# Splitting and re-assigning the first steps of a two-layer transformer kernel's opening

## The chip, the cores and the metric

The kernel runs on one core of a Trainium2 chip. A core has a matrix engine (PE, with its weight loads shown apart as PEld), a vector engine (DVE), a scalar engine (ACT), a general engine (POOL) and a sync engine (SP) that issues most DMA transfers. Each engine executes its own instructions in the order in which they stand in the program, and waits on semaphores for the others. The metric is the device time of one execution in microseconds (us). Before the change it is 1490.43 us, the median of three runs (1489.74 to 1490.46).

## The reference, cut to what matters

The reference runs two layers over 1024 latent and 256 context tokens of width 1024, in fp32: a windowed grouped-query attention, then a latent attention. Only the very beginning of the first layer matters here: each token row is normalised by its root mean square, scaled and shifted channel by channel, and multiplied with the input weights.

```
shift_x, scale_x, gate_x = adaln(c, ada_w[i], ada_b[i])
hx = rms_norm(x, norm_g[i]) * (1.0 + scale_x[:, None]) + shift_x[:, None]
hc = rms_norm(ctx, norm_g[i]) * (1.0 + scale_c) + shift_c
...
q, k, v, g = jnp.split(h @ w_in, [A_WIDTH, A_WIDTH + A_KV_WIDTH, A_WIDTH + 2 * A_KV_WIDTH], axis=-1)
```

`silu(c) @ w` inside `adaln` gives the per-channel scale and shift, so that no row can be finished before part of `ada_w` has been loaded and multiplied.

## The kernel before, in words

Every fp32 operand of a large product is kept as two parts in a format that PE multiplies in one pass: a **high part** (the value cast) and a **low part** (the value less its high part). A product is then three matmuls: high by high, low by high, high by low.

Tokens are handled in five pairs of 128-token tiles: pair 0 is the context, pairs 1 to 4 the latent tokens. A pair and a group of two 128-channel blocks make one group of the opening; there are 20 of them, and for each the opening does the same things:

- `square(p)` (ACT, L863): the sum of squares of each of the two tiles, 128x1024 each, into an accumulator. `norm(p)`: a small DVE operation (L867) and a small power on POOL (L868) make the reciprocal root from both sums at once. `scale(p, j, eng)`: tile j is multiplied by it on DVE (L875) or on ACT (L873).
- `turn(p, b, bank)` (PE, L882): four transposes bring two channel blocks of the pair into one PSUM bank.
- `h_part(p, b, hi)`: DVE applies scale and shift from the bank into SBUF, one channel block of 256 columns at a time (L890, two per group); then `hi`, a cast by ACT or POOL, writes the high part of both blocks (L892, 128x512).
- `h_low(p, b, eng)` (L897): DVE or POOL subtracts to get the low part.
- `v_part(p, b)`: eight matmuls with the high part (L906), then four with the low part (L911), into the bank of the pair.

Between them stand pieces of the scale and shift computation: `ada_mm` (PE, L839), `ada_copy` (ACT, L844), `ada_cols` (PE, L849, and three small DVE operations on L328 and L331), and the cutting of the first weight block (`w0_cut`, L929 and L930). SP loads in a fixed order: context, `ada_w`, the first piece of weights, the four tiles of pairs 1 and 2, the second piece of weights, more of `ada_w`, then pair 3 and the rest.

The opening is written out by hand in program order and is issued exactly so; no planner reorders it. One further rule sets waits: instructions of two different engines that touch the same PSUM bank, even if both only read it, and even if they read different columns, are put in program order by a semaphore.

Of the kernel before, what the change touches and what calls it, by code (L numbers as in the profile page):

```python
# [14 lines left out]
AF = mybir.ActivationFunctionType  # L15
ALU = mybir.AluOpType
# [4 lines left out]
D = 1024  # L21
# [5 lines left out]
EPS = 1e-6  # L27
# [190 lines left out]
def kernel(ctx: ExitStack, tc: tile.TileContext, t, out, dbg=None):  # L218
    plan = Plan()
    nc = Recorder(tc.nc, plan)  # L220
# [75 lines left out]
    mhalf = sm(1)  # L296
# [563 lines left out]
    def square(p):  # L860
        junk = V[:, 8:10].rearrange("p a b c -> p (a b c)") if p > 2 else PB[:, 3:5, :].rearrange("p a b -> p (a b)")
        for j in range(2):
            nc.scalar.activation(junk, xn[p][0][:, j], AF.Square, accum_out=xn[p][1][:, j : j + 1])  # L863

    def norm(p):
        _, sq, st = xn[p]
        nc.vector.tensor_scalar(st[:, 0:2], sq[:, 0:2], 1.0 / D, EPS, ALU.mult, ALU.add)  # L867
        nc.gpsimd.tensor_tensor(st[:, 2:4], st[:, 0:2], mhalf.to_broadcast([128, 2]), ALU.pow)  # L868
# [8 lines left out]
    def turn(p, b, bank):  # L877
        tbank[p, b] = ps = shp(PB[:, bank, :], 2, 256)
        for kk in range(2):
            for j in range(2):  # L880
                c0 = (2 * b + kk) * 128
                nc.tensor.transpose(ps[:, kk, j * 128 : j * 128 + 128], xn[p][0][:, j, c0 : c0 + 128], ident)  # L882

    def h_part(p, b, hi=nc.scalar.copy):
        w = 1 if p == 0 else 0
        ps, h = tbank[p, b], shp(hr.next(), 2, 256)
        for kk in range(2):
            k = 2 * b + kk
            sa, sb = ada0.A[:, k, w : w + 1], ada0.B[:, k, w : w + 1]
            nc.vector.tensor_scalar(h[:, kk], ps[:, kk], sa, sb, ALU.mult, ALU.add)  # L890
        ks = slice(2 * b, 2 * b + 2)
        hi(hT[p][:, 0, ks, :], h)  # L892
        hs[p, b] = h
# [5 lines left out]
    def v_part(p, b):  # L899
        h, W = hT[p], wt[0]  # L900
        for j in range(2):
            js = slice(j * 128, j * 128 + 128)
            o = PB[:, p, j * 256 : j * 256 + 256]
            for k in (2 * b, 2 * b + 1):
# [70 lines left out]
    h_part(0, 0, nc.gpsimd.tensor_copy)  # L975
    square(1)
    norm(1)
    h_low(0, 0, nc.vector)
    for j in range(2):
        scale(1, j, nc.vector)  # L980
    v_part(0, 0)
    turn(1, 0, 7)
    square(2)
    norm(2)
    h_part(1, 0)
    scale(2, 0, nc.vector)
    scale(2, 1, nc.scalar)
# [7 lines left out]
    h_part(2, 0)  # L995
# [10 lines left out]
    h_part(0, 1, nc.gpsimd.tensor_copy)  # L1006
# [3 lines left out]
    h_part(1, 1)  # L1010
# [1100 lines left out]
```

## Time and profile before

| what | value |
|---|---|
| time, median of three runs | 1490.43 us |
| the profiled execution's own time | 1488.73 us |
| its span, first to last instruction | 1486.9 us |
| mean granted clock of PE | 0.997 |
| PE busy | 1462.6 us, 98% of the span |
| DVE, ACT, POOL busy | 1064.1, 733.5, 810.4 us |
| stretch 14 to 24 us: PE busy, granted clock | 7.05 of 10 us, 0.66 |
| stretch 28 to 36 us: PE busy | 6.99 of 8 us |
| stretch 48 to 60 us: PE busy | 12.00 of 12 us |

A row of the timeline gives start, duration, engine, line, operation, what it writes and reads, shape and count (consecutive instructions of one kind are merged); in brackets stands the idle time of that engine before it and what ended it. A row of groups gives the count, the busy time in us, the mean of one in ns, and the idle time before it. A row of the stretches gives the length, each engine's busy time, PE's granted clock and the DMA engines' share. A row of the waits reads: who waited, for whom, us in total, how often, the longest.

### The profile page before, as it was taken

What the parts mean: (1) busy time and instruction counts of PE and PEld (TensorE: products, weight loads), DVE (VectorE), ACT (ScalarE), POOL (GpSimd) and SP (SyncE); (2) the same over time, 40 slices, a digit from 0 to 9 for tenths busy, and PEclk for the clock granted to TensorE, in tenths of its full rate; (3) what the DMA queues carried; (4) which work ended last, traced back from release to release, by engine and by line L of the source; (5) the groups of instructions that cost most, each with busy time, mean ns of one, the idle gap of its engine ahead of it and who ended that gap; (6) DMA issues with size and microseconds to landing.
All of it is one profiled execution on the core that took longest, in us unless ns stands there. A gap on an engine that the chain in (4) does not pass through costs nothing.

```text
span 1486.9 us, 25072 instructions
## 1 busy us (share of the span) xinstructions
PE 1462.6 (98%) x9036; PEld 1188.3 (80%) x9036; DVE 1064.1 (72%) x2029; ACT 733.5 (49%) x1397; POOL 810.4 (55%) x735
## 2 busy tenths in 40 slices
PE   6999999999999999999999999999999999999998
PEld 4888888888888888888888888766777767876687
DVE  3787789738778888878988777666576466566764
ACT  4421222359888878876554432443454344444321
POOL 2563366346454444456300240798788788789371
PEclk9999999999999999999999999999999999999999
DMA  9545644673343333336444566011122212120442
GB/s 336 170 171 170 212 150 169 208 223 114 121 144 119 98 101 98 100 100 229 119 120 119 169 234 207 21 41 53 47 63 70 62 47 61 54 68 28 151 152 86
DMA packets 146964, 186.01 MB, mean 125 GB/s; under 512 B 12812, under 2 KB 100492, under 8 KB 146840
## 3 DMA queue, kind: packets, MB, share of 16 engines
q1 hardware_dynamic: 141864, 177.75, 37.7%
q10 hardware_dynamic: 4976, 6.66, 1.3%
q8 instruction: 71, 1.16, 0.3%
q14 instruction: 53, 0.43, 0.1%
HBM read 134.02 MB, written 46.15 MB: 121 GB/s over the span
## 4 chain that ended last, share of the span: by engine, by line
PE 49%; DVE 2%; issue 1%; DMA 0%; POOL 0%; ACT 0%; POOLq 0%; DVEq 0%; ACTq 0%
PE PB L1788 13%; PE PB L1811 9%; PE PB L285 7%; PE PB L287 7%; PE PB L286 7%; PE PB L1754 5%; PE PB L1822 1%; DVE arena_r L281 1%; DMA arena_r<-arena_f 0%; PE PB L1768 0%; DVE arena_f L1327 0%; DVE krF L1760 0%; DVE arena_f L1236 0%; DVE arena_f L1329 0%; DVE arena_f L1328 0%
## 5 line engine op out<-in xcount | busy, mean ns | idle before, releaser
L285 PE MATMUL PB<-arena_r 128*128 128x512 f32 (+2 forms) x1200 | 439.4, 366 | 1.3 <-DVE arena_f L1236 1.3
L286 PE MATMUL PB<-arena_r 128*128 128x512 f32 (+2 forms) x1200 | 433.7, 361 | 0.1
L287 PE MATMUL PB<-arena_r 128*128 128x512 f32 (+2 forms) x1200 | 433.3, 361 | 0.0
L1804 POOL TENSOR_TENSOR arena_f<-arena_f 128x1024 f32<-128x1024 f32 x120 | 285.9, 2382 | 8.2
L285 PEld LDWEIGHTS PB<-arena_r 128*128 128x128 f32 x1200 | 226.3, 189 | 45.7 <-issue 9.0
L287 PEld LDWEIGHTS PB<-arena_r 128*128 128x128 f32 x1200 | 226.3, 189 | 33.7
L286 PEld LDWEIGHTS PB<-arena_r 128*128 128x128 f32 x1200 | 226.5, 189 | 32.2 <-POOL arena_r L281 0.8
L1788 PE MATMUL PB<-arena_r 64*128 64x512 f32 (+1 forms) x1600 | 229.6, 395 | 0.0
L1798 ACT ACTIVATE arena_f<-PB 128x1024 f32<-128x1024 f32 x160 | 164.5, 1028 | 112.0 <-PE PB L1788 84.0
L1760 DVE TENSOR_REDUCE krF<-PB 128x1 f32<-128x512 f32 (+1 forms) x264 | 167.0, 678 | 65.7 <-PE PB L1754 65.6
L1788 PEld LDWEIGHTS PB<-arena_r 64*128 64x128 f32 (+1 forms) x1600 | 179.4, 185 | 14.7 <-issue 5.2
L704 DVE CUSTOM_DVE_ANT_0 arena_f<-PB,arena_f,small 128x256 f32<-128x256 f32 (+1 forms) x288 | 148.1, 525 | 51.9 <-PE PB L698 33.3
L280 ACT CAST arena_r<-PB 128x512 fp32r<-128x512 f32 (+2 forms) x207 | 115.3, 564 | 113.2 <-PE PB L287 73.3
L281 DVE TENSOR_TENSOR arena_r<-PB,arena_r 128x512 fp32r<-128x512 f32 (+2 forms) x207 | 134.3, 661 | 34.7 <-ACT arena_r L280 34.1
L1811 PE MATMUL PB<-arena_f 128*64 128x512 f32 x640 | 145.9, 595 | 0.0
L281 POOL TENSOR_TENSOR arena_r<-arena_f,arena_r 128x512 fp32r<-128x512 f32 (+1 forms) x64 | 87.9, 1388 | 102.9 <-ACT arena_r L280 89.4
L710 ACT ACTIVATE arena_f<-arena_f,small 128x640 f32<-128x640 f32 (+2 forms) x160 | 119.1, 745 | 15.8 <-DVE small L704 13.6
L280 ACT CAST arena_r<-arena_f 128x512 fp32r<-128x512 f32 (+1 forms) x142 | 82.2, 611 | 87.3 <-PE PB L287 28.3
L507 DVE SCALAR_TENSOR_TENSOR arena_f<-arena_f,small 128x512 f32<-128x512 f32 x98 | 114.0, 1208 | 10.9 <-DMA arena_f<-ada_w 10.6
L737 PE MATMUL PB<-arena_r 128*128 128x512 f32 x336 | 118.6, 429 | 0.0
L1754 PE MATMUL PB<-arena_r 64*128 64x512 f32 (+1 forms) x768 | 114.2, 355 | 0.1
L727 PE MATMUL PB<-ident,arena_f 128*128 128x128 f32 x672 | 108.6, 272 | 0.1
(215 smaller groups left out, 2087.2 us busy)
## 6 DMA issues: line engine op xcount, KB each, us to landing
arena_f<-ada_w SPq DMA_DIRECT2D x96, 256.0 KB, 4.1
arena_r<-q_d SPq DMA_DIRECT2D x160, 128.0 KB, 2.8
arena_f<-a_w_in SPq DMA_DIRECT2D x40, 256.0 KB, 3.9
arena_f<-b_w_in SPq DMA_DIRECT2D x36, 256.0 KB, 2.9
arena_f<-x SPq DMA_DIRECT2D x16, 512.0 KB, 5.8
q_d<-arena_f SPq DMA_DIRECT2D x16, 512.0 KB, 3.0
arena_r<-qn_d SPq DMA_DIRECT2D x16, 512.0 KB, 5.0
g_d<-arena_f ACTq DMA_DIRECT2D x20, 256.0 KB, 3.7
```

The costliest lines, as they stand in the source:

```text
L280: nc.scalar.copy(hi, src)
L281: (lo_eng or nc.vector).tensor_sub(lo, src, hi.bitcast(F32))
L285: nc.tensor.matmul(o, ah, bh, start=first, stop=False)
L286: nc.tensor.matmul(o, al, bh, start=False, stop=False)
L287: nc.tensor.matmul(o, ah, bl, start=False, stop=last)
L704: nc.vector.tensor_tensor_reduce(o, S, mk, -A_SCALE, prev, ALU.add, ALU.min, mx)
L1754: nc.tensor.matmul(bank[:, o : o + n], self.q[r, s, bs], k[r, 0, n0 : n0 + n], start=s == 0, stop=s == 2)
L1760: nc.vector.reduce_max(self.mxp[:, e, b : b + 1, i], bank[:, 0:n], AX.X)
L1788: nc.tensor.matmul(PB[:, b + e, :], k[r, s, cs], q[r, sq], start=i == 0, stop=i == 4)
L1798: nc.scalar.activation(E, PB[:, b : b + 2, :], AF.Exp)
L1804: eng.tensor_add(acc, acc, E)
L1811: nc.tensor.matmul(PB[r, 7, :], Vq[:, c, h, :], E[:, e], start=c == 0, stop=c == NT - 1)
```

## The change

Five edits, all in the opening:

1. `square` and `norm` can be called for one tile. For pairs 1 and 2 the power is now taken tile by tile, each tile is scaled as soon as its own power is there, and both tiles of pair 2 are scaled on DVE (the second was on ACT).
2. `turn` issues the two transposes of the first tile before those of the second; `v_part` issues the high matmuls channel block by channel block.
3. The high part of group (0, 0) is cast on POOL in two halves, one channel block each.
4. Four high parts no longer go through SBUF: ACT computes scale and shift itself, with the scale and shift columns as its operands, from the PSUM bank into the high part (`hi is None`), one channel block at a time, for (1, 0), (0, 1) and (1, 1) with two instructions each. DVE still computes the same from the same bank into SBUF, for the low part. Before, (1, 0) and (1, 1) were cast by ACT and (0, 1) by POOL.
5. The high part of (2, 0) is cast by POOL instead of ACT.

Three calls of `h_part` pass `None`, which makes six ACT instructions.

```diff
-    def norm(p):
+    def norm(p, j=0, n=2):
         _, sq, st = xn[p]
-        nc.vector.tensor_scalar(st[:, 0:2], sq[:, 0:2], 1.0 / D, EPS, ALU.mult, ALU.add)
-        nc.gpsimd.tensor_tensor(st[:, 2:4], st[:, 0:2], mhalf.to_broadcast([128, 2]), ALU.pow)
+        nc.vector.tensor_scalar(st[:, j : j + n], sq[:, j : j + n], 1.0 / D, EPS, ALU.mult, ALU.add)
+        nc.gpsimd.tensor_tensor(st[:, 2 + j : 2 + j + n], st[:, j : j + n], mhalf.to_broadcast([128, n]), ALU.pow)
...
-        for kk in range(2):
-            for j in range(2):
+        for j in range(2):
+            for kk in range(2):
                 c0 = (2 * b + kk) * 128
                 nc.tensor.transpose(ps[:, kk, j * 128 : j * 128 + 128], xn[p][0][:, j, c0 : c0 + 128], ident)
 
-    def h_part(p, b, hi=nc.scalar.copy):
+    def h_part(p, b, hi=nc.scalar.copy, parts=1):
...
             nc.vector.tensor_scalar(h[:, kk], ps[:, kk], sa, sb, ALU.mult, ALU.add)
+            if hi is None:
+                nc.scalar.activation(hT[p][:, 0, k], ps[:, kk], AF.Identity, bias=sb, scale=sa)
+            elif parts == 2:
+                hi(hT[p][:, 0, k], h[:, kk])
         ks = slice(2 * b, 2 * b + 2)
-        hi(hT[p][:, 0, ks, :], h)
+        if hi and parts == 1:
+            hi(hT[p][:, 0, ks, :], h)
...
-    h_part(0, 0, nc.gpsimd.tensor_copy)
-    square(1)
-    norm(1)
-    h_low(0, 0, nc.vector)
+    h_part(0, 0, nc.gpsimd.tensor_copy, 2)
     for j in range(2):
+        square(1, [j])
+        norm(1, j, 1)
+        if j == 0:
+            h_low(0, 0, nc.vector)
         scale(1, j, nc.vector)
     v_part(0, 0)
     turn(1, 0, 7)
-    square(2)
-    norm(2)
-    h_part(1, 0)
+    square(2, [0])
+    norm(2, 0, 1)
+    square(2, [1])
+    h_part(1, 0, None)
     scale(2, 0, nc.vector)
-    scale(2, 1, nc.scalar)
+    norm(2, 1, 1)
+    scale(2, 1, nc.vector)
     w0_cut(1)
...
     h_low(1, 0, nc.vector)
     v_part(1, 0)
...
-    h_part(2, 0)
+    h_part(2, 0, nc.gpsimd.tensor_copy)
...
-    h_part(0, 1, nc.gpsimd.tensor_copy)
+    h_part(0, 1, None)
     square(3)
     h_low(0, 1, nc.vector)
     norm(3)
-    h_part(1, 1)
+    h_part(1, 1, None)
     h_low(1, 1)
```

Where instructions now stand is seen at three places. In these rows stand the line, the operation, what is written and read (`PB` is PSUM, `arena_f` and `arena_r` are SBUF, `small` holds the columns), the shape and the semaphores waited for. Up to L890 the line numbers are the same in both kernels; further down they are five higher in the changed one: L892 there is the new ACT instruction, L897 the 512-column cast and L902 the low part.

The first place is DVE from the scaling of pair 1 to the low part of group (1, 0). Before:

```order
L875 TENSOR_SCALAR arena_f<-arena_f,small 128x1024 [waits DMAHW0_49,Pool_49]
L875 TENSOR_SCALAR arena_f<-arena_f,small 128x1024 [waits DMAHW1_49]
L867 TENSOR_SCALAR small<-small 128x2 [waits Activation_49]
L890 TENSOR_SCALAR arena_f<-PB,small 128x256 [waits PE_49]
L890 TENSOR_SCALAR arena_f<-PB,small 128x256
L875 TENSOR_SCALAR arena_f<-arena_f,small 128x1024 [waits DMAHW2_49,Pool_49]
L897 TENSOR_TENSOR arena_r<-arena_f,arena_r 128x512 [waits Activation_49]
```

The same place now:

```order
L875 TENSOR_SCALAR arena_f<-arena_f,small 128x1024 [waits DMAHW0_49,Pool_49]
L867 TENSOR_SCALAR small<-small 128x1 [waits Activation_49]
L875 TENSOR_SCALAR arena_f<-arena_f,small 128x1024 [waits DMAHW1_49,Pool_49]
L867 TENSOR_SCALAR small<-small 128x1 [waits Activation_49]
L890 TENSOR_SCALAR arena_f<-PB,small 128x256 [waits PE_49]
L890 TENSOR_SCALAR arena_f<-PB,small 128x256 [waits Activation_49]
L875 TENSOR_SCALAR arena_f<-arena_f,small 128x1024 [waits DMAHW2_49,Pool_49]
L867 TENSOR_SCALAR small<-small 128x1
L875 TENSOR_SCALAR arena_f<-arena_f,small 128x1024 [waits DMAHW3_49,Pool_49]
L902 TENSOR_TENSOR arena_r<-arena_f,arena_r 128x512 [waits Activation_49]
```

Between the two scalings of each pair a small operation and a wait for POOL have come in; the second L890 has a new wait for ACT; and the low part of (1, 0) now stands behind a second scaling of pair 2.

The second place is ACT from the high part of (2, 0) to that of (2, 1). Before:

```order
L892 CAST arena_r<-arena_f 128x512 [waits DVE_49]
L844 COPY arena_f<-PB 98x256 [waits PE_49]
L863 ACTIVATE arena_r,small<-arena_f 128x1024 [waits DMAHW5_49]
L863 ACTIVATE arena_r,small<-arena_f 128x1024 [waits DMAHW6_49,Activation_49]
L892 CAST arena_r<-arena_f 128x512 [waits DVE_49]
L873 ACTIVATE arena_f<-arena_f,small 128x1024 [waits Activation_49,Pool_49]
```

The same place now:

```order
L844 COPY arena_f<-PB 98x256 [waits PE_49]
L892 ACTIVATE arena_r<-PB,small 128x256 [waits DVE_49,PE_49]
L892 ACTIVATE arena_r<-PB,small 128x256 [waits DVE_49]
L863 ACTIVATE arena_r,small<-arena_f 128x1024 [waits DMAHW5_49]
L863 ACTIVATE arena_r,small<-arena_f 128x1024 [waits DMAHW6_49,Activation_49]
L892 ACTIVATE arena_r<-PB,small 128x256 [waits DVE_49] x2
L873 ACTIVATE arena_f<-arena_f,small 128x1024 [waits Activation_49,Pool_49]
```

The cast of (2, 0) has left ACT, and the two instructions of (0, 1) have come in ahead of the squares of pair 3.

The third place is DVE from group (0, 1) to group (1, 1). Before:

```order
L890 TENSOR_SCALAR arena_f<-PB,small 128x256 [waits DVE_49]
L890 TENSOR_SCALAR arena_f<-PB,small 128x256
L897 TENSOR_TENSOR arena_r<-arena_f,arena_r 128x512 [waits Pool_49]
L867 TENSOR_SCALAR small<-small 128x2 [waits Activation_49]
L890 TENSOR_SCALAR arena_f<-PB,small 128x256 [waits PE_49]
```

The same place now:

```order
L890 TENSOR_SCALAR arena_f<-PB,small 128x256 [waits DVE_49]
L890 TENSOR_SCALAR arena_f<-PB,small 128x256 [waits Activation_49]
L902 TENSOR_TENSOR arena_r<-arena_f,arena_r 128x512 [waits Activation_49]
L867 TENSOR_SCALAR small<-small 128x2 [waits Activation_49]
L890 TENSOR_SCALAR arena_f<-PB,small 128x256 [waits PE_49]
L890 TENSOR_SCALAR arena_f<-PB,small 128x256 [waits Activation_49]
```

The order of these instructions is the same; the second L890 of each group now waits for ACT, and the L867 of pair 3 waits, as before, for squares that now stand behind two more ACT instructions.

12 lines of the change are left out of this document (6 added, 6 removed).

## The prediction

> **What bounds the kernel now.** I read the page first, then the stretches, then the timeline of the first 45 us, where the brackets show what each engine waited for.
>
> ```profile
> PE 1462.6 (98%) x9036; PEld 1188.3 (80%) x9036; DVE 1064.1 (72%) x2029; ACT 733.5 (49%) x1397; POOL 810.4 (55%) x735
> ```
> ```profile
> 14.00:24.00 10.00, 7.05 (x45) 4.40 (x44) 5.74 (x14) 5.92 (x11) 4.25 (x5) 0.66 1.07 375
> 28.00:36.00 8.00, 6.99 (x53) 6.31 (x54) 5.33 (x13) 5.53 (x10) 3.89 (x5) 1.00 1.08 369
> 36.00:48.00 12.00, 11.67 (x112) 9.72 (x111) 7.01 (x16) 6.73 (x13) 9.20 (x8) 1.00 0.77 244
> 48.00:60.00 12.00, 12.00 (x118) 10.41 (x117) 8.23 (x18) 5.06 (x10) 3.66 (x3) 1.00 0.40 141
> ```
>
> PE bounds all but the opening. From 48 us on it has no hole to speak of, so an opening that reaches 45 us later ends later by as much. Between 14 and 36 us PE waits for the conversion of the first tokens (2.95 us idle up to 24, 1.01 from 28 to 36), longest for the cast of group (0, 0), as the timeline of the first part shows. That is where the change can win; what it can lose is any lateness of DVE, ACT and POOL that PE sees.
>
> **The prices.** For ACT's scale and shift from the bank, for POOL's half cast, for a one-column power, for DVE's affine step and for a tile's scaling there are rows of the same form (groups; the fifth is the durations of one line):
>
> ```profile
> L1461 ACT ACTIVATE arena_f<-PB,small 128x256 f32<-128x256 f32 x20 | 10.2, 562 | 9.7 <-POOL krF L404 5.0 <-issue 2.8 <-DVE arena_f L1462 1.8
> L763 POOL CAST arena_r<-arena_f 128x256 fp32r<-128x256 f32 x39 | 15.5, 398 | 2.5
> L1117 POOL TENSOR_TENSOR small<-small 128x1 f32<-128x1 f32 x10 | 5.9, 595 | 2.8 <-DVE small L1116 2.8
> L890 DVE TENSOR_SCALAR arena_f<-PB,small 128x256 f32<-128x256 f32 x23 | 11.4, 540 | 6.6 <-PE PB L882 3.7 <-POOL arena_r L897 2.6
> L875 DVE TENSOR_SCALAR arena_f<-arena_f,small x7: 742/747/1750, 10.3 to 39.3; 128x1024 f32<-128x1024 f32 x7
> ```
>
> That two engines take turns at a bank is also seen in this trace, where a later stage shares one between DVE and ACT:
>
> ```profile
> 709.34 0.54 DVE L1462 TENSOR_SCALAR arena_f<-PB,small 128x256 f32<-128x256 f32 x1
> 709.96 1.02 ACT L1461 ACTIVATE arena_f<-PB,small 128x256 f32<-128x256 f32 x2 [0.83 <-POOL krF L404]
> ```
>
> ACT starts 0.08 us after DVE's end. In the changed order DVE's second half waits for ACT's first half and ACT's second half for DVE's second. One group from the bank is then a chain: 0.54, 0.08 + 0.56, 0.03 + 0.54, 0.08 + 0.56. DVE is free after 1.75 us (1.00 before) and the high part is whole after 2.39 us (about 1.65 before: 22.02 to 23.67 below). Its first half is there after 1.18 us.
>
> **First part: group (0, 0), a gain.**
>
> ```profile
> 16.48 1.00 DVE L890 TENSOR_SCALAR arena_f<-PB,small 128x256 f32<-128x256 f32 x2
> 17.54 0.61 POOL L892 CAST arena_r<-arena_f 128x512 fp32r<-128x512 f32 x1 [1.19 <-DVE arena_f L890]
> 18.20 2.08 PE L906 MATMUL PB<-arena_r 128*128 128x256 f32 x8 [2.43 <-POOL arena_r L892]
> 18.24 0.68 DVE L897 TENSOR_TENSOR arena_r<-arena_f,arena_r 128x512 fp32r<-128x512 f32 x1
> 18.41 1.08 POOL L868 TENSOR_TENSOR small<-small 128x2 f32<-128x2 f32 x1 [0.27 <-DVE small L867]
> 19.53 1.42 DVE L875 TENSOR_SCALAR arena_f<-arena_f,small 128x1024 f32<-128x1024 f32 x2 [0.60 <-POOL small L868]
> 20.93 1.06 PE L882 MATMUL PB<-ident,arena_f 128*128 128x128 f32 x4
> ```
>
> The first half of DVE's work ends at 16.48 + 0.54 = 17.02; POOL's half cast runs 17.09 to 17.49, and PE starts at 17.54 instead of 18.20, 0.66 us earlier. The other half is cast by 17.94, and nothing stops PE after that.
>
> **Second part: pair 1 tile by tile, a loss.** The power of the first tile can start on POOL only behind the two half casts, at 18.01, beside DVE's low part (17.97 to 18.65). In the row above the power beside that low part took 1.08 us and ended 0.56 us after it; so 19.21. (Unhindered it would be 18.01 + 0.60 = 18.61, my other bound.) Scaling: 19.25 to 20.00. Then what is new: the second tile's small operation stands behind this scaling (20.08; the small ones take 0.16 and overlap by 0.08), its power costs 0.07 + 0.60 (20.75), its scaling 0.03 + 0.75: 21.53, where before both were scaled by 19.53 + 1.42 = 20.95. Two transposes remain for PE, 0.64 us (1.06 less two starts of 0.21): 22.22 instead of 21.99. The early start of PE is used up, and `h_part(1, 0)` begins at 22.26 instead of 22.02.
>
> [...]
>
> **Third part: group (1, 0) and pair 2, the first large loss.**
>
> ```profile
> 22.02 0.99 DVE L890 TENSOR_SCALAR arena_f<-PB,small 128x256 f32<-128x256 f32 x2 [1.00 <-PE PB L882]
> 23.05 0.62 ACT L892 CAST arena_r<-arena_f 128x512 fp32r<-128x512 f32 x1 [2.34 <-DVE arena_f L890]
> 23.28 0.10 PEld L839 LDWEIGHTS PB<-arena_f,small 128*2 128x2 f32 x6 [0.43 <-DMA arena_f<-ada_w]
> 23.71 0.69 DVE L897 TENSOR_TENSOR arena_r<-arena_f,arena_r 128x512 fp32r<-128x512 f32 x1
> 24.14 1.22 PE L906 MATMUL PB<-arena_r 128*128 128x256 f32 x8
> 25.20 0.65 PE L911 MATMUL PB<-arena_r 128*128 128x256 f32 x4
> ```
>
> PE cannot start these high matmuls before 24.14 in either kernel, since it waits for `ada_w` from memory until 23.28 just ahead of them; the DMA engines are full (share 1.07 above), so nothing lands sooner. The halves of the high part at 23.44 and 24.65 hold it up little. But DVE, free at 22.26 + 1.75 = 24.01, now has ahead of the low part: scaling (24.68), small operation (24.76), a wait for POOL's power (25.43), second scaling (26.21). The low part ends at 26.82 instead of 24.40, and PE's L911 starts at 26.87 instead of 25.20: **+1.67 us**. (26.3 with the unhindered power.) That ACT no longer scales a tile saves 1.14 us on an engine that was not waited for here.
>
> **Fourth part: group (2, 0) cast by POOL, a gain.**
>
> ```profile
> 26.21 1.04 PE L839 MATMUL PB<-arena_f,small 128*2 128x256 f32 x16
> 27.35 0.62 ACT L892 CAST arena_r<-arena_f 128x512 fp32r<-128x512 f32 x1 [2.12 <-DVE arena_f L890]
> 27.87 0.37 ACT L844 COPY arena_f<-PB 98x256 f32<-98x256 f32 x1
> 28.00 0.69 DVE L897 TENSOR_TENSOR arena_r<-arena_f,arena_r 128x512 fp32r<-128x512 f32 x1 [0.69 <-ACT arena_r L892]
> 28.29 0.63 PE L849 MATMUL PB<-small,arena_f 98*128 98x34 f32 x4 [0.45 <-ACT arena_f L844]
> ```
>
> The copy that PE waits for no longer stands behind the cast: it could start at 26.21 + 1.04 + 0.04 = 27.29, not 27.87, 0.58 us sooner. PE reaches `v_part(2, 0)` at +1.67 - 0.58 = **+1.09**; POOL's cast (0.61 for 0.62) is no later.
>
> **Fifth part: group (0, 1) and the squares of pair 3, the second loss.**
>
> ```profile
> 28.14 1.06 ACT L863 ACTIVATE arena_r<-arena_f 128x1024 fp32r<-128x1024 f32 x1
> 29.50 0.99 DVE L890 TENSOR_SCALAR arena_f<-PB,small 128x256 f32<-128x256 f32 x2
> 30.28 0.19 ACT L863 ACTIVATION_READ_ACCUMULATOR arena_r<-arena_f 128x1 f32 x1
> 31.81 0.16 DVE L867 TENSOR_SCALAR small<-small 128x2 f32<-128x2 f32 x1
> 31.88 0.99 DVE L890 TENSOR_SCALAR arena_f<-PB,small 128x256 f32<-128x256 f32 x2
> 33.61 1.29 POOL L897 TENSOR_TENSOR arena_r<-arena_f,arena_r 128x512 fp32r<-128x512 f32 x1 [0.86 <-ACT arena_r L892]
> 34.95 0.74 PE L911 MATMUL PB<-arena_r 128*128 128x256 f32 x4 [0.16 <-POOL arena_r L897]
> ```
>
> DVE's low part of (2, 0) ends 1.67 + 0.05 later, at 30.41, and with the small operations behind it `h_part(0, 1)` starts at 30.80 instead of 29.50. From the bank its high part is whole at 30.80 + 2.39 = 33.19. Only then comes ACT to the squares of pair 3, which before ran from 28.14 to 30.47 while POOL cast: 2.33 us, now to 35.43. DVE's small operation for pair 3 (31.81 before, without a wait) stands ahead of `h_part(1, 1)` and now waits for them, to 35.46; so `h_part(1, 1)` starts at 35.54 instead of 31.88: **+3.66**.
>
> **Sixth part: group (1, 1).** High part whole at 35.54 + 2.39 = 37.93, POOL's low part 0.08 + 1.29 later, 39.30, PE at 39.35 instead of 34.95: **+4.40 us**. Behind it stands PE's whole rest, and the next squares (pair 4) follow on ACT equally late.
>
> **The sum.** -0.66 used up, +1.67, -0.58, then +3.3 more: +4.4. Bounds: low, the power unhindered (-0.6), ACT's five steps on this chain at 0.37 (the copy in the fourth part) instead of 0.56 (-0.95), and PE's 0.33 us of holes between 36 and 48 us given back, makes +2.5; high, +4.7 with 0.3 for POOL's low part beside DVE. The profiled execution, 1488.73 us, would become 1493.1; the median of the runs shown lies 1.70 above it, so I forecast 1490.43 + 4.4 = **1494.8 us**, with 1492.9 to 1495.2 as this case's own range.
>
> **Rivals.** *B, the clock falls as well.* PE would have little work from 35.0 to 39.35: four high matmuls twice, some 1.3 us in all.
>
> ```profile
> 13.75:17.16 3.41, 1.50 (x15) 0.71 (x13) 1.22 (x5) 1.70 (x4) 1.88 (x2) 1.00 1.03 411
> 17.16:20.58 3.42, 2.38 (x11) 2.38 (x12) 2.13 (x5) 3.14 (x6) 1.69 (x2) 0.50 1.06 368
> 713.50:716.91 3.41, 2.08 (x16) 1.82 (x15) 3.41 (x10) 1.70 (x7) 2.52 (x3) 1.00 0.45 164
> ```
>
> A stretch of 3.41 us with PE busy for 1.50 (44%) was followed by a granted clock of 0.50; one with 2.08 (61%) was not. Our hole lies near the first. At half clock the eight matmuls of a group took 2.08 us instead of 1.22, so 3.41 us do some 2.0 us of work: -1.4 for one such stretch, up to 2.7 for two as after 17.16, less where PE would wait anyway. Take +1.5: 1496.3 us. Against it: where the stretches fall is not known. [...]
>
> *C, part of it is given back.* ACT's and DVE's lateness is caught up in the groups up to 48 us, where DVE is busy 7.01 of 12 us. Then some 2.4 us stay: 1492.8 us. For it: DVE and ACT have room; against it, PE has only 0.33.
>
> *D, no loss.* If the chain at the bank and the squares were off PE's path, the gains would be left: 0.66 us at 17.54 and 0.58 at 27.29, of which the wait for `ada_w` swallows most of the first. That makes about -1.0, 1489.4 us. It decides if DVE's low parts of (1, 0) and (1, 1) end before PE's high matmuls do, at 25.2 and about 35. Against it are the waits in the program's own order. That the change does nothing at all is not open.
>
> **How the numbers follow.** A 0.42, B 0.38, C 0.13, D 0.07. The range 1492.0 to 1497.5 holds A, B up to its two stretches, and most of C. A measurement of this kernel tells about 0.2%, 3.0 us, from no change. Slower by more: nearly all of A and B, 0.78. Within it: C, most of D and the rest of A, 0.18. Faster by more: 0.04, as D alone with a clock that rises sooner could give.
>
> **What would show it.** In the profile of the changed kernel: L906 (now L911) at 17.5 for (0, 0); DVE and ACT alternating at L890 and L892, ACT near 0.56 us; a wait of DVE's L867 for the squares of pair 3 of some 1.5 us near 35; PE waiting 1.5 us or more near 25 to 27 and some 4 us in all between 31 and 39. If DVE's L867 does not wait there, A is wrong. A granted clock of 0.50 after 36 us shows B.

## The result, and the profile after

The changed kernel took 1493.23 us (median of seven runs, 1492.92 to 1495.56), beside 1489.74 us for the kernel before in the same session (seven runs, 1487.14 to 1490.46). The ratio is 1.0032, with a 95% interval of 1.0023 to 1.0042: slower by 0.32%, between 3.4 and 6.3 us (the medians are 3.5 us apart). The two longest of the seven, 1494.73 and 1495.56 us, are the two with the lowest mean granted clock of PE, 0.995; the others have 0.996 or 0.997. The profiled execution took 1493.23 us with a span of 1491.4 us, 4.5 us more than the span before. The forecast was 1494.8 us, 4.4 us more than before.

Engine busy times of the changed kernel, and three stretches of it (length, busy time of PE, PEld, DVE, ACT and POOL, PE's granted clock, DMA share):

```profile
PE 1466.7 (98%) x9036; PEld 1189.1 (80%) x9036; DVE 1063.9 (71%) x2032; ACT 734.2 (49%) x1399; POOL 810.2 (54%) x738
```
```profile
24.00:28.00 4.00, 2.83 (x26) 2.06 (x24) 2.40 (x3) 0.05 (x1) 1.54 (x2) 1.00 1.05 385
28.00:36.00 8.00, 6.65 (x56) 4.97 (x48) 4.35 (x11) 3.69 (x7) 1.52 (x3) 1.00 1.08 369
36.00:48.00 12.00, 10.72 (x68) 8.84 (x72) 4.85 (x10) 7.75 (x12) 6.15 (x6) 0.72 0.29 91
```

PE's busy time over the whole span is 4.1 us more for the same instructions: of its busy time in the first 60 us, 9.74 us (3.19, 3.13 and 3.42) lay in stretches at half clock, where before it was 5.79 (2.38 and 3.41). Three stretches changed. From 24 to 28 us PE now sits idle for 1.17 us (before 0.16), from 28 to 36 for 1.35 (before 1.01), and between 36 and 48 us it is idle for 1.28 and its granted clock is 0.72, where before it was idle for 0.33 at 1.00. From 48 to 60 us it is busy for 12.00 of 12 us, as before.

The timeline shows the chain of the forecast. The first two groups and pair 2, on PE, POOL and DVE:

```profile
17.41 2.08 PE L911 MATMUL PB<-arena_r 128*128 128x256 f32 x8 [1.66 <-POOL arena_r L894]
17.77 0.56 POOL L868 TENSOR_TENSOR small<-small 128x1 f32<-128x1 f32 x1
18.46 0.74 DVE L875 TENSOR_SCALAR arena_f<-arena_f,small 128x1024 f32<-128x1024 f32 x1
21.22 0.55 DVE L890 TENSOR_SCALAR arena_f<-PB,small 128x256 f32<-128x256 f32 x1 [0.47 <-PE PB L882]
...
24.26 1.28 POOL L935 TENSOR_TENSOR arena_r<-arena_f,arena_r 128x512 fp32r<-128x512 f32 x1
24.33 1.76 DVE L875 TENSOR_SCALAR arena_f<-arena_f,small 128x1024 f32<-128x1024 f32 x1 [0.66 <-POOL small L868]
26.02 0.68 DVE L902 TENSOR_TENSOR arena_r<-arena_f,arena_r 128x512 fp32r<-128x512 f32 x1
26.75 0.74 PE L916 MATMUL PB<-arena_r 128*128 128x256 f32 x4 [1.17 <-DVE arena_r L902]
...
29.42 0.63 PE L849 MATMUL PB<-small,arena_f 98*128 98x34 f32 x4
```

PE starts 0.79 us earlier than before (18.20), is 1.55 us late at the low matmuls of (1, 0) (before 25.20) and 1.13 late at L849 (before 28.29). Then the groups (0, 1) and (1, 1):

```profile
30.74 0.54 DVE L890 TENSOR_SCALAR arena_f<-PB,small 128x256 f32<-128x256 f32 x1
31.38 0.56 ACT L892 ACTIVATE arena_r<-PB,small 128x256 fp32r<-128x256 f32 x1 [2.01 <-DVE arena_f L890]
31.98 0.54 DVE L890 TENSOR_SCALAR arena_f<-PB,small 128x256 f32<-128x256 f32 x1 [0.69 <-ACT arena_r L892]
32.56 0.56 ACT L892 ACTIVATE arena_r<-PB,small 128x256 fp32r<-128x256 f32 x1 [0.61 <-DVE arena_f L890]
33.02 1.05 ACT L863 ACTIVATE arena_r<-arena_f 128x1024 fp32r<-128x1024 f32 x1
...
35.37 0.17 DVE L867 TENSOR_SCALAR small<-small 128x2 f32<-128x2 f32 x1 [1.53 <-ACT arena_r L863]
35.45 0.54 DVE L890 TENSOR_SCALAR arena_f<-PB,small 128x256 f32<-128x256 f32 x1
...
39.18 1.22 PE L916 MATMUL PB<-arena_r 128*128 128x256 f32 x4
```

DVE and ACT take turns at the bank, ACT reaches the squares of pair 3 at 33.02 instead of 28.14, DVE's small operation waits 1.53 us for them, and PE's low matmuls of (1, 1) start at 39.18 instead of 34.95: 4.23 us late. From the low matmuls of (1, 0) up to here forecast and trace differ by no more than 0.2 us on this path; ahead of that they differ by up to 1.04 us, as told below.

Behind it the trace goes another way. These are four of the stretches of 3.41 us at whose edges the granted clock changed (at 17.19, 20.60, 37.67 and 44.50 us in the first 60 us of this trace):

```profile
24.02:27.43 3.41, 2.24 (x19) 1.70 (x14) 2.37 (x2) 0.03 (x1) 1.52 (x2) 1.00 1.06 389
34.26:37.67 3.41, 1.56 (x12) 1.11 (x10) 1.66 (x4) 2.12 (x5) 0.71 (x1) 1.00 1.05 331
37.67:41.08 3.41, 3.13 (x13) 2.83 (x14) 1.06 (x3) 3.38 (x6) 2.56 (x2) 0.50 0.07 24
41.08:44.50 3.42, 3.42 (x17) 3.18 (x16) 1.08 (x3) 1.15 (x3) 1.74 (x2) 0.50 0.00 0
```

PE was busy for 1.56 of the 3.41 us from 34.26, and the two stretches behind ran at half clock. A landmark at 57 us, the same four matmuls, tells what PE's lateness has become; before, and changed:

```profile
56.61 0.53 PE L849 MATMUL PB<-small,arena_f 98*128 98x34 f32 x4
```
```profile
62.84 0.53 PE L849 MATMUL PB<-small,arena_f 98*128 98x34 f32 x4
```

PE is 6.23 us late there, 2.0 more than at the low matmuls of (1, 1), and the span ends only 4.5 us later. So 1.7 us were given back somewhere behind 57 us. Set side by side in their order, PE's instructions of the two traces show where: the lateness falls by 0.6 us near 683 us and by 0.9 us near 714 us, and the last 0.4 us lie behind PE's last instruction. In the kernel before, PE at the first of these places, and DVE and PE at the second:

```profile
683.90 0.66 PE L1454 MATMUL PB<-ident,arena_f 128*128 128x128 f32 x4 [0.75 <-DVE arena_f L1462]
```
```profile
711.46 0.69 DVE L1327 TENSOR_TENSOR arena_f<-arena_r 128x512 f32<-128x512 f32 x1 [1.58 <-DMA arena_r<-arena_f]
```
```profile
715.43 0.37 PE L285 MATMUL PB<-arena_r 128*128 128x288 f32 x1 [1.33 <-DVE arena_f L1236]
```

In the changed kernel PE has no wait at the first place; the second (L1335 is L1327 there):

```profile
716.35 0.69 DVE L1335 TENSOR_TENSOR arena_f<-arena_r 128x512 f32<-128x512 f32 x1 [0.71 <-DMA arena_r<-arena_f]
```
```profile
720.31 0.37 PE L285 MATMUL PB<-arena_r 128*128 128x288 f32 x1 [0.48 <-ACT arena_f L1211]
```

At the second place DVE waits for a transfer, and PE for DVE (in the changed kernel, for ACT). PE's instruction is only 4.88 us late, and its wait 0.85 us shorter. That made three questions for the experiments: which edit costs what, whether the clock is to blame for 2.0 us, and whether the give-back belongs to the change.

### The profile page after: what moved, and what is told of

Same layout as the page of the kernel before. It is cut to its first block, busy times and chain, and to the rows that moved or that the text cites. A ratio compares the mean times of both kernels' runs of the same rounds, so it can differ in the third digit from the quotient of the medians.

```text
span 1491.4 us, 25082 instructions
## 1 busy us (share of the span) xinstructions
PE 1466.7 (98%) x9036; PEld 1189.1 (80%) x9036; DVE 1063.9 (71%) x2032; ACT 734.2 (49%) x1399; POOL 810.2 (54%) x738
## 4 chain that ended last, share of the span: by engine, by line
PE 49%; DVE 2%; issue 1%; DMA 0%; POOL 0%; ACT 0%; POOLq 0%; DVEq 0%; ACTq 0%
PE PB L1796 13%; PE PB L1819 9%; PE PB L285 7%; PE PB L286 7%; PE PB L287 7%; PE PB L1762 5%; PE PB L1830 1%; DVE arena_r L281 1%; DMA arena_r<-arena_f 0%; PE PB L1776 0%; DVE krF L1768 0%; DVE arena_f L1244 0%; DVE arena_f L1337 0%; DVE arena_f L1335 0%; DVE arena_f L1336 0%
## 5 line engine op out<-in xcount | busy, mean ns | idle before, releaser
L285 PE MATMUL PB<-arena_r 128*128 128x512 f32 (+2 forms) x1200 | 439.4, 366 | 0.5 <-ACT arena_f L1211 0.5
L285 PEld LDWEIGHTS PB<-arena_r 128*128 128x128 f32 x1200 | 226.3, 189 | 45.2 <-issue 9.0
```

The lines of the kernel that those rows point to most:

```text
L285: nc.tensor.matmul(o, ah, bh, start=first, stop=False)
```

## The experiments

Each kernel was profiled once and, E8 apart, timed against the kernel before. "Late" is the start of PE's L849 near 57 us less 56.61, "end" the span less 1486.9 us; "half clock" counts the whole stretches at 0.50 that began after 24 us.

| kernel | low matmuls of (1, 1) at | late | half clock | end | ratio to before (95%) |
|---|---|---|---|---|---|
| before | 34.95 | 0 | 0 | 0 | 1 |
| changed | 39.18 | 6.23 | 2 | 4.5 | 1.0032 (1.0023 to 1.0042) |
| E1: (0, 1) cast by POOL again | 37.88 | 2.98 | 0 | 2.3 | 1.0022 (1.0013 to 1.0031) |
| E2: low part of (1, 0) earlier | 39.38 | 5.54 | 1 | 5.0 | 1.0031 (1.0019 to 1.0044) |
| E3: eight more matmuls in the hole | 39.48 | 4.58 | 0 | 4.7 | 1.0038 (1.0023 to 1.0053) |
| E4: before, PE alone delayed | 35.02 | 5.40 | 0 | 4.3 | 1.0032 (1.0019 to 1.0045) |
| E5: ACT's two ahead of DVE's two | 38.53 | 4.71 | 1 | 4.4 | 1.0030 (1.0020 to 1.0039) |
| E6: no high part from the bank | 36.71 | 1.76 | 0 | 0.5 | 1.0003 (0.9994 to 1.0012) |
| E7: only the edits that gain | 34.40 | -0.54 | 0 | -1.4 | 0.9998 (0.9989 to 1.0007) |
| E8: before once more | 34.75 | -0.20 | 0 | -0.9 | one run |
| E9: before with pair 2's edit alone | 37.13 | 2.20 | 0 | 1.3 | 1.0014 (1.0005 to 1.0024) |
| E10: before with (0, 1) from the bank alone | 37.11 | 2.67 | 1 | 3.0 | 1.0028 (1.0017 to 1.0039) |
| E11: (1, 1) cast by ACT again | 40.73 | 6.88 | 2 | 6.9 | 1.0038 (1.0023 to 1.0053) |

Ratios against the same few runs of before resolve about 0.1%, 1.5 us; the column "late" is one profile each, and two profiles of the kernel before differ by 0.20 us in it. Earlier in the opening single profiles differ by more: at L849 near 28 us E8 is 0.20 and E10, up to there the kernel before, 0.46 us ahead of the first profile. How long PE runs at half clock ahead of it differs too: until 23.99 us in the first profile, 22.78 in E8 and 22.07 in E10.

### E1: the high part of (0, 1) cast by POOL again

```
-    h_part(0, 1, None)
+    h_part(0, 1, nc.gpsimd.tensor_copy)
```

> The changed kernel with one edit undone: the high part of (0, 1) is cast by POOL again, as before. Theory (the squares of pair 3 behind ACT's two instructions of (0, 1) hold DVE up): the squares can then run from about 29.4, behind the copy, to 31.8 instead of 33.0 to 35.4, so the small operation of pair 3 no longer waits 1.5 us and h_part(1, 1) starts near 33.2 instead of 35.45; PE's low matmuls of (1, 1), at 39.18 in the changed kernel, start near 37.0, 2.2 us sooner. PE is then busy for more of the stretch 34.3 to 37.7 and the granted clock should stay 1.00 after it, which would give another 2 us: about 4 us sooner at 60 us. Rival (taking turns at the bank is the whole loss, the squares none): the low matmuls of (1, 1) stay within 0.5 us of 39.2 and the clock falls as in the changed kernel.

In the timeline of E1, POOL at (0, 1):

```profile
32.35 0.53 POOL L474 MEMSET arena_f<- 97x512 f32 x1 [2.21 <-PE PB L882]
32.82 0.61 POOL L897 CAST arena_r<-arena_f 128x512 fp32r<-128x512 f32 x1
```

Measured: the low matmuls of (1, 1) at 37.88, 1.30 us sooner than in the changed kernel; no stretch at half clock after 24 us; 3.25 us sooner at 57 us. The direction is the theory's and the small operation no longer waits for the squares, but 1.30 is not 2.2: the chain started 0.5 us later (probably since E1's PE ran at half clock until 23.48, the changed kernel's only until 20.60), and a memset that I had not counted (0.53 us) stands on POOL ahead of the cast. The rival, that the squares do no harm, is out. By the times the kernel gained 0.1% on the changed one, within what the intervals leave open.

### E2: the low part of (1, 0) ahead of the second tile's scaling

```
     scale(2, 0, nc.vector)
+    h_low(1, 0, nc.vector)
     norm(2, 1, 1)
...
-    h_low(1, 0, nc.vector)
     v_part(1, 0)
```

> The changed kernel with the low part of (1, 0) moved on DVE ahead of the small operation and the scaling of the second tile of pair 2. Theory (what is late there is only DVE's order): the low part ends near 24.3 instead of 26.7 and PE's low matmuls of (1, 0) start near 25.4 instead of 26.75. The second tile's scaling, then behind it, ends near 26 if POOL leaves DVE alone, near 26.9 if DVE waits for POOL's low part of the weights beside it as it did in the changed kernel (1.76 us for a scaling that took 0.74 elsewhere); by the first PE is 1.3 us sooner at the transposes of (2, 0), now at 27.33, by the second only 0.4. Rival (the whole 1.55 us at (1, 0) comes back in the end): 1.3 us or more sooner at 60 us.

In the timeline of E2, DVE and PE:

```profile
24.45 0.69 DVE L902 TENSOR_TENSOR arena_r<-arena_f,arena_r 128x512 fp32r<-128x512 f32 x1
...
25.87 1.77 DVE L875 TENSOR_SCALAR arena_f<-arena_f,small 128x1024 f32<-128x1024 f32 x1 [0.66 <-POOL small L868]
```
```profile
27.70 0.44 PE L882 MATMUL PB<-ident,arena_f 128*128 128x128 f32 x2 [0.42 <-DVE arena_f L875]
```

The low part was ready at 25.14 instead of 26.70. PE's low matmuls followed only at 26.42 (25.4 was expected), behind high matmuls that ran partly at half clock, which lasted until 26.14 here. The scaling moved behind the low part again took 1.77 us, and the second half of the transposes waits for it and starts at 27.70 (all four stood at 27.33 in the changed kernel). The lateness has only changed its place: at the low matmuls of (1, 1) PE is where it was (39.38 and 39.18). The rival is out. The 0.7 us won at 57 us came with one slow stretch instead of two.

### E3: matmuls that fill the hole

```
+        if i == 4:
+            for _ in range(8):
+                nc.tensor.matmul(PB[:, 3, 0:256], hT[0][:, 0, 0, 0:128], wt[0][:, 0, 0, :], start=True, stop=True)
         v_part(p, q)
```

> The changed kernel with eight more matmuls (128x256, results unused, a bank that nothing else touches then) on PE ahead of v_part(1, 1), where PE waits 1.56 us; they take about 1.1 us. Theory (the clock falls to 0.50 at 37.7 since PE was busy for only 1.56 of the 3.41 us before, and costs 2.0 us by 48 us): with 2.6 us of work in that stretch the clock stays 1.00; the low matmuls of (1, 1) still start near 39.2, but at 60 us PE is about 2.0 us ahead of the changed kernel, and the end about 1.5 to 2 us sooner although PE does more work. Rival (the clock falls for another reason, or PE makes up the slow stretch anyway): the clock shows 0.50 again, or it stays 1.00 and PE gains less than 0.5 us.

PE's timeline of E3 (L1029 are the eight), and the stretch of the clock in which most of them fell:

```profile
35.14 1.19 PE L1029 MATMUL PB<-arena_r 128*128 128x256 f32 x8
```
```profile
35.69:39.10 3.41, 2.11 (x14) 1.50 (x12) 2.71 (x6) 2.16 (x4) 1.66 (x2) 1.00 0.63 199
39.10:42.51 3.41, 3.03 (x28) 2.86 (x32) 0.55 (x3) 2.79 (x6) 1.93 (x3) 1.00 0.01 4
```

The stretch from 35.69 had 2.11 us of work and no slow one followed; without the 0.64 us of the eight that fell into it (35.69 to 36.33) it would have had 1.47, less than the 1.56 after which the clock fell in the changed kernel. From the low matmuls of (1, 1) to the landmark the lateness stayed (4.53 and 4.58 us), where in the changed kernel it grew from 4.23 to 6.23. So the clock does cost the 2.0 us up to 57 us. The table agrees: from the low matmuls of (1, 1) to the landmark the lateness stays within 0.05 us where no slow stretch follows (E1, E3, E6, E7, E9) and grows by 0.5 to 1.1 us with one (E2, E5, E10, and E11, whose other one came earlier). The other half of the expectation failed: the end was no sooner (4.7 and 4.5 us late; ratios 1.0038 and 1.0032). Nothing was given back behind 57 us: PE lost another 0.6 us between 300 and 340 us, for a reason that stays open, and gained 0.4 near 714. So the times of E3 don't show the 2.0 us.

### E4: PE alone made late

47 such matmuls ahead of `v_part(2, 1)` in the kernel before (`if i == 5`, `range(47)`).

> The kernel before with 47 more matmuls (128x256, results unused, an idle bank) on PE ahead of v_part(2, 1), near 39 us: PE alone is late by 47 x 0.133 = 6.2 us from there on, at full clock. It measures what a lateness of PE at 60 us is worth at the end. Theory (part is given back near 680 and 715 us, where PE waits for other engines that are not late): PE is 6.2 us late at 340 us and 4.5 to 5 us at the end, as in the changed kernel, and the holes of 0.75 us at 683 and 1.33 us at 714 shrink. Rival (a lateness at 60 us passes whole to the end, and the profile of the changed kernel ended 1.7 us sooner by chance): 6.2 us at the end.

PE's timeline of E4, and DVE at the place where it waited for a transfer (L1330 is L1327 here):

```profile
35.96 5.88 PE L1021 MATMUL PB<-arena_r 128*128 128x256 f32 x47
```
```profile
715.08 0.68 DVE L1330 TENSOR_TENSOR arena_f<-arena_r 128x512 f32<-128x512 f32 x1
```

PE is 5.40 us late at 57 us, less than the 6.2 reckoned, since the matmuls took 0.12 us each and part of them filled PE's own waits. The end is 4.3 us late. DVE no longer waits for the transfer at all (before 1.58 us), and PE's wait at L285 is 0.31 us instead of 1.33. So in this profile the lateness does not pass whole to the end, and 1.1 us of it is gone near 714 us; E8 will show 0.5 us gone there with no edit at all. The wait at 683 us did not shrink here, so that part of the theory is not borne out.

### E5: ACT's two instructions ahead of DVE's two

```
+        if hi is None:
+            for k in (2 * b, 2 * b + 1):
...
+                nc.scalar.activation(hT[p][:, 0, k], ps[:, k - 2 * b], AF.Identity, bias=sb, scale=sa)
         for kk in range(2):
...
             nc.vector.tensor_scalar(h[:, kk], ps[:, kk], sa, sb, ALU.mult, ALU.add)
-            if hi is None:
-                nc.scalar.activation(hT[p][:, 0, k], ps[:, kk], AF.Identity, bias=sb, scale=sa)
-            elif parts == 2:
+            if hi and parts == 2:
```

> The changed kernel, but in the three groups whose high part comes from the bank ACT's two instructions stand ahead of DVE's two, instead of the four alternating. Theory (taking turns at the bank is part of the price, the place of the squares the other): a high part is whole 1.08 us after its bank is ready instead of 2.39, DVE's part about 1.0 us later than that. (0, 1): ACT 30.8 to 31.8, the squares of pair 3 from 31.9 to 34.2 instead of 33.0 to 35.4; (1, 1): high part whole near 35.3 instead of 37.8, DVE's part until 36.3, POOL's low part until 37.6, PE's low matmuls at 37.6 to 37.9 instead of 39.18. PE has work at 35, so the clock should fall for one stretch at most: at 60 us 1.3 to 3.5 us sooner than the changed kernel. Rival (only the squares count): the low matmuls of (1, 1) stay within 0.5 us of 39.2.

In the timeline of E5, ACT, DVE and POOL:

```profile
31.52 1.02 ACT L890 ACTIVATE arena_r<-PB,small 128x256 fp32r<-128x256 f32 x2 [1.43 <-DVE small L328]
...
34.66 1.00 ACT L890 ACTIVATE arena_r<-PB,small 128x256 fp32r<-128x256 f32 x2
...
35.70 0.99 DVE L894 TENSOR_SCALAR arena_f<-PB,small 128x256 f32<-128x256 f32 x2 [0.74 <-ACT arena_r L890]
...
36.84 1.64 POOL L904 TENSOR_TENSOR arena_r<-arena_f,arena_r 128x512 fp32r<-128x512 f32 x1 [1.09 <-DVE arena_f L894]
```

The high part of (1, 1) was whole at 35.66 instead of 37.76, as expected, but the low matmuls start at 38.53, between the two theories. The chain came to (0, 1) 0.8 us later than in the changed kernel (31.52 for 30.74), and now the low part is what is late: DVE is through 1.03 us behind ACT, and POOL's low part took 1.64 us beside DVE's scaling (1.28 in the changed kernel). Who took the first turn at the bank decided which of the two parts was late: the high part in the changed kernel, the low part here. It did not remove the lateness (4.71 us at 57 us for 6.23).

### E6: nothing taken from the bank

```
-    h_part(1, 0, None)
+    h_part(1, 0)
...
-    h_part(0, 1, None)
+    h_part(0, 1, nc.gpsimd.tensor_copy)
...
-    h_part(1, 1, None)
+    h_part(1, 1)
```

> The changed kernel without the instructions from the bank: the high parts of (1, 0), (0, 1) and (1, 1) are cast from SBUF by ACT, POOL and ACT, as before; pairs 1 and 2 stay tile by tile, and (2, 0) is cast by POOL. Theory (the instructions from the bank cost the larger part of the loss, pair 2 on DVE the rest): the low part of (1, 0) still ends near 26 and PE's low matmuls there start 0.5 to 1.5 us later than before; the low matmuls of (1, 1) start near 36.3 to 37 (before 34.95, changed 39.18, with only the POOL cast of (0, 1) undone 37.88); the clock stays 1.00 after 27; at 60 us PE is 1 to 2 us behind the kernel before, and the time about 1490 us. Rival (pair 2 tile by tile is the larger part): 3 us or more behind at 60 us.

Three groups take their high part from the bank, these three; the "four" in the fourth edit is a slip. As expected: the low matmuls of (1, 1) at 36.71, 1.76 us late at 57 us, and no difference in time that can be measured (1.0003). The instructions from the bank account for 4.5 of the 6.23 us in this comparison, the slow stretches that they bring among them.

### E7: only the edits that gain

The kernel before with the high part of (0, 0) cast in two halves, PE's new order in `turn` and `v_part`, and (2, 0) cast by POOL:

```
-    h_part(0, 0, nc.gpsimd.tensor_copy)
+    h_part(0, 0, nc.gpsimd.tensor_copy, 2)
...
-    h_part(2, 0)
+    h_part(2, 0, nc.gpsimd.tensor_copy)
```

> The kernel before with only those edits that the traces show as gains: the high part of (0, 0) in two halves, PE's new order in the transposes and the high matmuls, and the high part of (2, 0) on POOL. PE waits 0.45 us for the copy at 28.29 in the kernel before and at most 1 us more up to 36 us, so the most that can be won is about 1 us. Theory: PE starts near 17.5 instead of 18.2, which the wait for ada_w until 23.3 swallows; the copy is 0.5 us sooner; at 60 us PE is 0.3 to 1 us ahead; the time is the same within what can be measured. Rival (the order channel block by channel block or POOL's extra work costs something): 0.5 us or more behind at 60 us.

PE in the timeline of E7:

```profile
30.68 1.22 PE L911 MATMUL PB<-arena_r 128*128 128x256 f32 x8 [0.98 <-POOL arena_r L897]
```

PE started L849 at 27.12, 1.17 us sooner than before, without a wait for the copy; 0.54 us are left at 57 us. Part of that is not the edits': PE ran at half clock only until 20.47 us here, and E10, without any of these edits, was 0.46 us ahead at the same place. In time it equals the kernel before (0.9998) and is faster than the changed kernel. What holds PE next is the cast of (0, 1).

### E8: the kernel before, profiled again

> The kernel before, unchanged, profiled a second time. The stretches of 3.41 us in which the clock is granted began at 13.75, 13.78, 13.24, 12.48, 11.8 and 10.5 us in the profiles so far, and DVE's wait for the transfers near 711 us was 1.58, 0.71, 1.45, 1.21 and 0 us. Theory (both depend on the execution and not on the kernel): here too they differ from the first profile of this kernel, the stretches by tenths of a us or more, the wait by 0.3 us or more, and PE differs by up to 1.5 us at 60 us and at the end. Rival (both are fixed by the kernel): stretches at 13.7, a wait of 1.5 to 1.6 us, PE within 0.2 us of the first profile.

DVE and PE near 711 us in E8:

```profile
710.72 0.69 DVE L1327 TENSOR_TENSOR arena_f<-arena_r 128x512 f32<-128x512 f32 x1 [1.02 <-DMA arena_r<-arena_f]
```
```profile
714.69 0.37 PE L285 MATMUL PB<-arena_r 128*128 128x288 f32 x1 [0.80 <-DVE arena_f L1236]
```

The wait for the transfer is 1.02 us here and was 1.58, and PE gains 0.5 us on the first profile at that place without any change of the kernel. The stretches of the clock began at 12.54 instead of 13.75. So both vary with the execution. Of the 1.7 us given back in the first comparison, 0.7 are found again between two profiles of one kernel (-0.20 at 57 us, -0.9 at the end). All the other eleven profiles gain on the first profile near 714 us too, by 0.15 to 1.06 us, the early E7 (0.69) as much as the late ones. So it is the first profile that lost time there; the gain does not grow with the lateness.

### E9 and E10: one part of the change alone, in the kernel before

E9:

```
-    square(2)
-    norm(2)
+    square(2, [0])
+    norm(2, 0, 1)
+    square(2, [1])
     h_part(1, 0)
     scale(2, 0, nc.vector)
-    scale(2, 1, nc.scalar)
+    norm(2, 1, 1)
+    scale(2, 1, nc.vector)
```

> The kernel before with only the third part of the change: pair 2's power tile by tile and both its scalings on DVE. Theory (DVE's order alone makes the low part of (1, 0) late): behind the first scaling, which ended at 23.7, come the small operation, POOL's power and a second scaling that POOL's low part of the weights holds to 1.76 us, so the low part ends near 26.8 and PE's low matmuls of (1, 0) start near 26.9 instead of 25.2; at 60 us PE is 1.5 to 2.3 us behind the kernel before; the clock stays 1.00 from 27 on. Rival (the lateness at (1, 0) is made up in the groups behind it, where PE waits 1 us up to 36 us): under 0.7 us behind at 60 us.

In the timeline of E9, POOL, DVE and PE:

```profile
24.81 1.27 POOL L935 TENSOR_TENSOR arena_r<-arena_f,arena_r 128x512 fp32r<-128x512 f32 x1
24.88 1.75 DVE L875 TENSOR_SCALAR arena_f<-arena_f,small 128x1024 f32<-128x1024 f32 x1 [0.67 <-POOL small L868]
...
27.29 0.74 PE L916 MATMUL PB<-arena_r 128*128 128x256 f32 x4 [1.81 <-DVE arena_r L902]
```

2.09 us late at the low matmuls of (1, 0), 2.20 at 57 us, and a time 0.14% above before. The third part is a loss of its own, and nothing makes it up in the groups behind. The rival is out.

E10 takes only `h_part(0, 1, None)` into the kernel before.

> The kernel before with only one high part taken from the bank by ACT, that of (0, 1), in two instructions that alternate with DVE's. Theory (the fifth part stands alone: the squares of pair 3 now start behind them): DVE's group (0, 1) starts at 29.5 as before, ACT is through at 31.9, the squares run until 34.2, the small operation of pair 3 waits for them, h_part(1, 1) starts near 34.3 instead of 31.9 and PE's low matmuls of (1, 1) near 37.4 instead of 34.95; at 60 us PE is 2 to 2.5 us behind, 4 if the clock falls as well. Rival (the squares hold nobody up, the loss needs the lateness of pair 2): under 0.7 us behind at 60 us.

In the timeline of E10, DVE:

```profile
33.67 0.17 DVE L867 TENSOR_SCALAR small<-small 128x2 f32<-128x2 f32 x1 [1.53 <-ACT arena_r L863]
```

The small operation of pair 3 waits 1.53 us, as in the changed kernel, although here nothing was late ahead of it. The low matmuls of (1, 1) are 2.16 us late, PE 2.67 us at 57 us with one slow stretch, and the time is 0.28% above before. Of the two parts tried alone in the kernel before, this single word costs more.

### E11: (1, 1) cast by ACT again

```
-    h_part(1, 1, None)
+    h_part(1, 1)
```

> The changed kernel with only the high part of (1, 1) cast from SBUF by ACT again. Theory (the sixth part's price is the turn taking at the bank, 0.7 us): h_part(1, 1) still starts near 35.5, behind the squares, DVE is through at 36.5, the cast at 37.1, POOL's low part at 38.4, PE's low matmuls start near 38.5 instead of 39.18. PE has no work between 35.1 and 37.1, so the clock falls as in the changed kernel; at 60 us 0.5 to 1 us sooner than that. Rival (the instructions from the bank are the whole loss at (1, 1)): the low matmuls of (1, 1) at 37 or sooner.

DVE in the timeline of E11, and two stretches of its clock:

```profile
37.66 0.99 DVE L890 TENSOR_SCALAR arena_f<-PB,small 128x256 f32<-128x256 f32 x2
```
```profile
23.98:27.39 3.41, 1.68 (x15) 1.02 (x11) 2.75 (x4) 0.94 (x2) 1.79 (x2) 1.00 1.06 390
27.39:30.81 3.42, 3.21 (x20) 2.07 (x24) 1.15 (x3) 0.00 (x0) 0.03 (x1) 0.50 1.07 390
```

From the start of `h_part(1, 1)` to the low matmuls (40.73) it took 3.07 us, in the changed kernel 3.73 (35.45 to 39.18): taking turns at this bank costs 0.66 us, as expected. But the absolute times missed by 2.2 us. Of these 0.85 were there at the low matmuls of (1, 0) already (27.60 for 26.75). Behind them the clock adds to it. Here the stretches lay so that one of them took in PE's hole at (1, 0), with 1.68 us of work, and the next ran at half clock; this hole is in the changed kernel too (1.17 us), where the stretch around it held 2.24 us of work and nothing followed. So what these two holes cost went with how they lay against the stretches, and the kernel does not place those: they began at 13.75 and 12.54 us in two profiles of the kernel before.

## Why the prediction was right, and where its sum was right by luck

**The forecast held**: slower, 1494.8 us against 1493.23, and +4.4 us against a ratio that says +3.4 to +6.3. (The upper end of its own range, 4.7 above 1490.43, is 1495.1 and not 1495.2.)

**The price of taking turns.** Held, though the row behind it does not show it cleanly: the wait of ACT at 709.96 is put down to POOL and not to DVE. In the changed kernel ACT and DVE follow each other at the bank after 0.10, 0.04 and 0.04 us (forecast 0.08, 0.03 and 0.08).

**First part, (0, 0).** Held: PE started at 17.41 (forecast 17.54), and the wait for `ada_w` swallowed the gain.

**Second part, pair 1.** Failed. The forecast put POOL's first power beside DVE's low part and took its long price, ending at 19.21. It ran from 17.77 to 18.33. It began 0.08 us ahead of the low part (17.85 to 18.54), and neither took longer than elsewhere in this trace (0.56 us, beside 0.55 at 19.35; 0.69, beside 0.68 at 26.02). The bound called unhindered (18.61) was the right one. `h_part(1, 0)` started at 21.22, not 22.26.

**Third part, (1, 0).** The end held, 26.75 for 26.87, but by two errors that cancel. The chain started 1.04 us sooner, and the second scaling took 1.76 us instead of the 0.75 of the sum, with POOL's low part of the weights (24.26 to 25.54) beside it: it started 0.07 us behind POOL's instruction and took 1.02 us longer than the same scaling alone (0.74). E9 shows the same pair, 1.75 us.

**Fourth part, (2, 0).** Held: the lateness fell from 1.55 to 1.13 us at L849, 0.42 of the 0.58 forecast.

**Fifth and sixth part.** Held within 0.2 us at every step: `h_part(0, 1)` at 30.74 (30.80), the high part whole at 33.12 (33.19), the squares done at 35.35 (35.43), `h_part(1, 1)` at 35.45 (35.54), the low matmuls at 39.18 (39.35). E10 shows the fifth part alone, E11 the price of the turns at the bank in the sixth.

**The signs.** DVE's wait of 1.5 us for the squares came (1.53), and so did the clock of 0.50. PE's waits came smaller than forecast: 1.17 us between 24 and 28 us for "1.5 us or more", and 2.43 us idle between 31 and 39 for "some 4 us", since PE's high matmuls and transposes are spread over that time.

**The step that failed is the choice of the likeliest case**, A, in which the clock stays at 1.00. By its own test, "a granted clock of 0.50 after 36 us shows B", the profiled execution was case B: two stretches cost 2.0 us, as E3 shows up to 57 us (the text took 1.5 and named 2.7 as the most). And 1.7 us less came out at the end, not caught up until 48 us, as C had it, but near 683 us, near 714 us and behind PE's last instruction. In the profiled execution 4.23 + 2.0 - 1.7 made 4.5, beside a sum of 4.4 that had neither of the last two terms. The 4.23 was reckoned; that the total agrees so well is luck.

**The first paragraph's rule**, that an opening late by x at 45 us ends late by x, looks refuted by 6.23 us that became 4.5, but the runs don't show that. The profile compared with is itself one that lost time near 714 us. Measured from E8 instead, the other eleven gain or lose up to 1.0 us between 57 us and the end, 0.1 on average, and the latest of them, E11, falls back by another 0.7. E4, made to test the rule, gives back 0.4 by this measure. So these single profiles show no give-back that goes with the lateness; the rule holds to within about 1 us, which varies with the execution.

**Rival D**, no loss, is excluded by E9 and E10, each slower than before by itself.

## What to carry to other kernels

A second engine at the same PSUM bank saves a cast but coupled two queues here (E10: a wait of 1.53 us, and PE 2.67 us late at 57 us with one slow stretch, for one group): price it by what stands behind both instructions on both engines (here the squares of the next pair and the small operation that waits for them), not by its own 0.56 us. A tile moved from a free engine to the one on the path costs its whole chain there, its small operation, its wait and what a neighbour adds included (2.20 us at 57 us in E9, where the scaling took 1.75 us instead of 0.74). And a lateness of a few us in an opening is not a fixed sum: a hole of 1.56 us in PE came to cost 2.0 us more, through two slow stretches of the clock, and places later on where PE waits for others shift the end by up to 1 us from one execution to the next. Whoever compares two single profiles should profile the kernel before twice.

## What the runs showed of the hardware that was not expected

**The clock's stretches.** The stretches read are 3.41 us long, and the first one counted began at 13.75, 13.78, 13.24, 12.48, 11.8 and 10.5 us in the profiles of before, changed and E1 to E4, and at 12.54 in E8, so the same kernel met them at different places (13.75 and 12.54). How much work decided can be bounded closely. Of the stretches at full clock between there and 60 us, six were read that held 1.88 us of PE work or less: 1.50 (before), 1.46 and 1.56 (changed), 1.68 (E11) and 1.88 (E2) were followed by 0.50, 1.77 (E1) was not. None of those read with more was: 1.91 (E2), 2.11 (E3), 2.24 (changed) and above, nor the one with 2.08 at 713.5 us (before). Ahead of PE's first matmul it was otherwise: before, the stretch from 3.51 to 6.92 us held no work and was followed by 1.00. The way back asked for more: at half clock, 2.38 (before) and 3.13 us of work (changed) were followed by another such stretch, 3.19 (changed), 3.21 (E11), 3.41 (before) and 3.42 (changed) by full clock. The two edges, in the stretches of E2 (full clock, then half) and of E1 (the one exception, 1.77 us of work and full clock behind it):

```profile
32.96:36.38 3.42, 1.91 (x12) 1.48 (x12) 1.31 (x3) 2.71 (x6) 0.55 (x1) 1.00 1.10 351
36.38:39.79 3.41, 1.88 (x11) 1.47 (x12) 2.12 (x4) 2.80 (x5) 1.55 (x3) 1.00 0.48 155
39.79:43.20 3.41, 3.41 (x18) 3.41 (x18) 1.08 (x3) 2.23 (x5) 1.85 (x2) 0.50 0.00 0
```
```profile
23.48:26.89 3.41, 1.77 (x15) 1.11 (x14) 2.75 (x4) 1.07 (x2) 1.79 (x2) 1.00 1.08 382
```

So 56% of a stretch (1.91 of 3.42) kept the clock in E2 and 55% (1.88 of 3.41) did not, though 52% did in E1; and 94% (3.19) brought it back in the changed kernel, where 92% (3.13) did not.

**A scaling beside POOL.** DVE's scaling of 128x1024 took 1.75 to 1.77 us in every profile quoted in which POOL's subtraction of 128x512 started 0.07 us ahead of it, and 0.74 alone. In E5 it was the other way round: there the scaling began at 36.61, 0.23 us ahead of POOL's subtraction, and took its 0.74 us, while the subtraction took 1.64 us instead of 1.28.
